# The spatial weight sums of an encoder kernel become a chain of their own, apart from the layer norm

## The chip, the cores and the metric

The kernel runs on one core of one Trainium2 chip. The metric is the device time of one execution in microseconds (us); lower is better. The five engines named in the text are PE (TensorE, the matrix multiply), DVE (VectorE, elementwise work and reductions), ACT (ScalarE, activation functions and copies), POOL (GpSimd, used here almost only to issue transfers) and SP (SyncE, used to issue transfers). Each engine works through its own list of instructions in order: an instruction that waits holds up all that stands behind it on that engine. A transfer (DMA) is issued from the list of an engine and then runs by itself; whoever needs its result waits for its landing.

## The reference: what is computed

A trunk of two residual layers over 512 tokens of 1024 channels. Each layer normalises its input, projects it once, runs three mixers in parallel (a gated linear recurrence, a spatial gating unit, a windowed attention), gates and projects each, and adds the merged result to its input. The change concerns the spatial gating unit alone:

```python
def spatial_gating(u, v, ln_g, ln_b, w_s, b_s):
    vn = layer_norm(v, ln_g, ln_b).reshape(B, L // SG_CHUNK, SG_CHUNK, SG_GROUPS, SG_GW)
    mixed = jnp.einsum('gts,bnsgc->bntgc', w_s, vn) + b_s.T[None, None, :, :, None]
    return u * mixed.reshape(B, L, SG_W)
```

The layer norm has a gain and a bias for each channel, and the mix over positions is linear. So the bias `ln_b` can be taken out of the mix: it contributes, for output position t of group g, `ln_b` times the sum over s of `w_s[g, t, s]`. These sums depend on weights only, not on the input.

## The kernel before, in words

The program is written in Python as one long stream of instructions with tiles taken from pools. A planner then orders the instructions of each engine: it keeps the data dependences, goes by the order of the program as a priority, and may let a later instruction go ahead when an earlier one would still wait by its own estimates. Instructions marked with `pin` keep their order among themselves. The weight loads on SP are pinned.

**The main stream.** PE goes through the weight blocks of a list (`PLAN`). A layer does, in order: the attention's queries (`nat_units(do_q)`, natural layout), its gates and keys, the recurrence's values (`nat_units(do_ia)`), the spatial unit's v (`nat_units(do_vb)`, four token blocks of 24 matmuls, each followed by a GELU of a Square and a Sigmoid on ACT and two operations on DVE, L1041 to L1044), and then for each of four heads h three blocks (query and two forget gates, `main_t`, 24 matmuls each, L520). Each weight block is split into a high part (ACT, L270) and a low part (DVE, L271) before PE may use it.

**Side work.** Between and in the middle of the blocks the program calls `advance(us)`. An advance hands out a credit of `us` to generators. Those in `sides` are served two at a time (`WIDTH = 2`), in turn, until the credit is used up; a generator that yields a number has used that much, and one that yields `None` waits for the next advance. Those in `timed` all run at every advance, ahead of the sides, up to their next `None`; what they use is taken from the same credit. So for a generator in `timed` each `None` is one advance, whatever else goes on. Each of the four token blocks of `do_vb` has two advances (one in its middle, one behind it), and so has each `main_t` block of the heads.

**The attention** is one generator in `sides` (`all_attention`). For each of four query blocks it makes scores on PE (L784 and L785, into the five `ps` slots of PSUM), reads each out with a fused operation on DVE (L786), takes the softmax (ACT L798 and L802, DVE L793 to L809), transposes it on DVE (L816), and sends it through DRAM with two transfers on POOL (L820 and L821). A second generator in `timed` multiplies it with the values eight advances later (L834).

**The layer norm and the weight sums** are one generator before, `ln_v`, which joins `sides` after `do_vb`. Its steps: load the spatial weights into `wsum` (L1054, SP, 256 KB), wait three advances, sum them over s on DVE (L1058), store the 512 sums into a small DRAM tile `sd` (L1060, POOL, 2 KB), load them back spread over all 128 partitions into `wsum` (L1061, POOL, 256 KB), take the mean and variance of v (L1067 and L1068, then the eleven small operations of `rstd`), wait for the next advance, normalise v (L1074), and last add the sums times the bias to the row of output biases `br` (L1079, four operations). `br` is read much later, in `spatial` (L1088). `wsum` holds one of seven slots of the tag `t2` from L1054 to L1079.

Of the kernel before, what the change touches and what calls it, by code (L numbers as in the profile page):

```python
# [18 lines left out]
ALU = mybir.AluOpType  # L19
# [3 lines left out]
P = 128  # L23
# [154 lines left out]
def hybrid_kernel(tc, x, wpk, brow, gainb, pvec, wsp, wsr, trig, amask, imask, out):  # L178
    nc = tc.nc
    from contextlib import ExitStack  # L180

    with ExitStack() as es:
        cp = es.enter_context(tc.tile_pool(name="const", bufs=1))
        wp = es.enter_context(tc.tile_pool(name="wts", bufs=4))
        sb = es.enter_context(tc.tile_pool(name="work", bufs=2))
        pp = es.enter_context(tc.tile_pool(name="psum", bufs=3, space=PSUM))
        dp = es.enter_context(tc.tile_pool(name="spill", bufs=1, space=bass.MemoryType.DRAM))
        build(nc, tc, cp, wp, sb, pp, dp, x, wpk, brow, gainb, pvec, wsp, wsr, trig, amask, imask, out)
# [6 lines left out]
def build(nc, tc, cp, wp, sb, pp, dp, x, wpk, brow, gainb, pvec, wsp, wsr, trig, amask, imask, out):  # L195
    V, S, G, E = nc.vector, nc.scalar, nc.gpsimd, nc.tensor
# [4 lines left out]
    def nm(s):  # L201
        cnt[0] += 1
        return f"{s}_{cnt[0]}"
# [4 lines left out]
    def t2(shape=(P, 512), dt=F32):  # L208
        return sb.tile(list(shape), dt, name=nm("t2"), tag="t2", bufs=N_T2)

    def small(n):
        return sb.tile([P, n], F32, name=nm("sm"), tag="small", bufs=24)
# [4 lines left out]
    def ps_side(shape=(P, 512), dt=F32):  # L217
        return pp.tile(list(shape), dt, name=nm("ps"), tag="ps", bufs=N_PS)
# [56 lines left out]
    def w_next():  # L275
        i = wi[0]
        wi[0] += 1
        w_conv_to(i + 1)
        return his[i], los[i]

    def w_ahead(n, eng=V):
        w_conv_to(wi[0] + n, eng=eng)
        w_load_to(OPERANDS[min(wi[0] + n, len(OPERANDS) - 1)][3])
# [40 lines left out]
    def rstd(ss, n, scale, order=free, small=small):  # L324

        v, y, a = small(n), small(n), small(n)
        order(V.tensor_scalar(v, ss, -0.5 * scale, -0.5 * EPS, ALU.mult, ALU.add))

        magic = float(0x5F3759DF - 0x40400000)
        order(V.tensor_scalar(y.bitcast(I32), v.bitcast(I32), -0.5, magic, ALU.mult, ALU.add))  # L330
        for _ in range(3):
            order(V.tensor_tensor(a, y, y, ALU.mult))
            order(V.tensor_tensor(a, a, v, ALU.mult))
            order(V.scalar_tensor_tensor(y, a, 1.5, y, ALU.add, ALU.mult))
        return y
# [17 lines left out]
    def gate_consts(l, eng):  # L353
        br = cp.tile([P, R_GQ], F32, name=nm("br"), tag="br", bufs=1)
        eng.dma_start(br, brow[l, :R_GQ].partition_broadcast(P))
        ws = cp.tile([P, 4, P], F32, name=nm("ws"), tag="ws", bufs=1)
        eng.dma_start(ws, wsp[l])
        return br, ws
# [118 lines left out]
    def nat_block(units, hth, htl, tb, mid=None, passes=IN_ORDER):  # L477

        po = ps_main()
        nat_part(po, units, hth, htl, tb, passes[:12], True, False)  # L480
        if mid is not None:
            mid()
        nat_part(po, units, hth, htl, tb, passes[12:], False, True)
        return po

    def nat_two(units, hth, htl, tbs, between):

        po = [ps_main() for _ in tbs]
        for n, (i, u) in enumerate(((0, 0), (0, 1), (1, 0), (1, 1), (0, 2), (1, 2), (0, 3), (1, 3))):
            passes = [(2 * u + k, j) for j in range(3) for k in range(2)]  # L490
            nat_part(po[i], units, hth, htl, tbs[i], passes, u == 0, u == 3)
            if n < 7:
                between(n)
        return po
# [32 lines left out]
    timed = []  # L527
# [31 lines left out]
    def advance(us):  # L559
        credit[0] += us  # L560
        waiting = []
        run_timed()
        while sides and credit[0] > 0:
            c = step(waiting)
            if c is None:
                break
            credit[0] -= c
        credit[0] = min(credit[0], 2.0 * us if sides else 0.0)
# [25 lines left out]
    for l in range(L):  # L594
# [4 lines left out]
        lnb = pvc[:, V_LNB + 4 * l : V_LNB + 4 * l + 4]  # L599
# [30 lines left out]
        def nat_units(handler, us, before=None, two=False, passes=IN_ORDER):  # L630
            un = [w_next() for _ in range(4)]
            for tb in range(NT):
                if before is not None:
                    before(tb)
                if two and tb < 2:
                    if tb == 1:
                        pos = nat_two(un, *hN, (0, 1), lambda n: advance(us / 2))
                        for i in range(2):
                            handler(i, pos[i])
                            advance(us / 2)  # L640
                    continue
                po = nat_block(un, *hN, tb, lambda: advance(us), passes if tb == 0 else IN_ORDER)
                if tb == NT - 1:
                    w_ahead(2)
                handler(tb, po)
                advance(us)
# [240 lines left out]
        br, ws = gate_consts(l, nc.sync)  # L887
# [160 lines left out]
                vg.append(m4((P, 2, 512)))  # L1048
            gelu(po, vg[tb // 2][:, tb % 2, :])

        def ln_v():

            wsum = t2((P, 4, P))
            nc.sync.dma_start(wsum, wsr[l])  # L1054
            for _ in range(3):
                yield None
            ss = small(4)
            V.tensor_reduce(ss, wsum, AX, ALU.add)  # L1058
            sd = dp.tile([4, P], F32, name=nm("sd"))
            G.dma_start(sd.rearrange("g t -> t g"), ss)  # L1060
            G.dma_start(wsum.rearrange("p g t -> p (g t)"), sd.rearrange("g t -> (g t)").partition_broadcast(P))  # L1061
            yield 0.5
            mv = small(8)
            mv2 = mv.rearrange("p (n c) -> p n c", c=2)
            for n in range(NT):
                st = small(6)
                V.bn_stats(st, vg[n // 2][:, n % 2, :])  # L1067
                V.bn_aggr(mv2[:, n, :], st)  # L1068
            r = rstd(mv2[:, :, 1], NT, 1.0)
            yield 2.5  # L1070
            yield None
            for n in range(NT):
                v = vg[n // 2][:, n % 2, :]
                V.tensor_scalar(v, v, mv2[:, n, 0:1], r[:, n : n + 1], ALU.subtract, ALU.mult)  # L1074
                yield 0.7

            for g in range(4):
                b = br[:, g * P : (g + 1) * P]
                V.scalar_tensor_tensor(b, wsum[:, g, :], lnb[:, g : g + 1], b, ALU.mult, ALU.add)  # L1079
            yield 0.5  # L1080

        def spatial(g):
            po = ps_side((P, 4, P))
            for n in range(NT):
                E.matmul(po[:, n, :], vg[n // 2][:, n % 2, g * P : (g + 1) * P], ws[:, g, :], start=True, stop=True)  # L1085
            y = t2((P, 4, P))
            bs = br[:, R_BS + g * P : R_BS + (g + 1) * P].unsqueeze(1).broadcast_to((P, 4, P))
            V.scalar_tensor_tensor(y, po, lng[:, g : g + 1], bs, ALU.mult, ALU.add)  # L1088
            u = uz[g // 2][:, g % 2, :]
            V.tensor_tensor(u, u, y.rearrange("p n t -> p (n t)"), ALU.mult)  # L1090
            yield 2.0
# [8 lines left out]

        glas = []
        lnv, spat = ln_v(), [spatial(g) for g in range(4)]
        nat_units(do_vb, 2.6)
        sides.append(lnv)
        for h in range(H):
# [449 lines left out]
```

## Time and profile before

| what | value |
|---|---|
| median of 3 runs | 1073.45 us (1072.95 to 1074.95) |
| the profiled execution's own time | 1074.03 us |
| its span, first to last instruction | 1072.3 us |
| PE busy | 1053.5 us, 98% |
| DVE busy | 819.2 us, 76% |
| ACT busy | 538.1 us, 50% |
| POOL busy | 118.5 us, 11% |
| mean granted TensorE clock | 0.995 |

All times inside the execution are counted from the start of the span. A row of instructions names the line of the kernel, the engine, the operation, and "out<-in" by tile names; `t` stands for a tile of the tag `t2`, `sm` for a small tile, `m` for a large one. In a row of a timeline the brackets at the end tell how long the engine was idle before it and what ended that idle time. In the view of stretches each engine's busy time stands beside the number of its instructions, followed by the clock that TensorE was granted (1.00 is full speed).

### The profile page before, as it was taken

What the parts mean: (1) busy time and instruction counts of PE and PEld (TensorE: products, weight loads), DVE (VectorE), ACT (ScalarE), POOL (GpSimd) and SP (SyncE); (2) the same over time, 40 slices, a digit from 0 to 9 for tenths busy, and PEclk for the clock granted to TensorE, in tenths of its full rate; (3) what the DMA queues carried; (4) which work ended last, traced back from release to release, by engine and by line L of the source; (5) the groups of instructions that cost most, each with busy time, mean ns of one, the idle gap of its engine ahead of it and who ended that gap; (6) DMA issues with size and microseconds to landing.
All of it is one profiled execution on the core that took longest, in us unless ns stands there. A gap on an engine that the chain in (4) does not pass through costs nothing.

```text
span 1072.3 us, 19220 instructions
## 1 busy us (share of the span) xinstructions
PE 1053.5 (98%) x7716; PEld 904.1 (84%) x7716; DVE 819.2 (76%) x1531; ACT 538.1 (50%) x819; POOL 118.5 (11%) x178
## 2 busy tenths in 40 slices
PE   8999989999999999999999999899999999999998
PEld 7888867787899998988878888677778999999886
DVE  6974789968888776578987567897698876775885
ACT  5344757654346543545533367575443464444442
POOL 0230011200001110110012201112000011101000
PEclk9999999999999999999999999899999999999999
DMA  8672446551327866783957424658213378557755
GB/s 311 177 220 95 157 142 231 193 160 60 103 75 159 206 192 162 168 251 112 301 167 231 133 79 157 206 178 260 76 59 120 79 188 219 165 138 193 239 154 141
DMA packets 54281, 178.55 MB, mean 167 GB/s; under 512 B 6320, under 2 KB 10928, under 8 KB 54192
## 3 DMA queue, kind: packets, MB, share of 16 engines
q1 hardware_dynamic: 28944, 100.77, 27.8%
q0 software_dynamic: 23520, 72.37, 26.9%
q10 hardware_dynamic: 1728, 4.20, 1.0%
q8 instruction: 60, 0.98, 0.4%
q14 instruction: 29, 0.24, 0.1%
HBM read 155.28 MB, written 22.02 MB: 165 GB/s over the span
## 4 chain that ended last, share of the span: by engine, by line
PE 79%; issue 12%; DVE 4%; DMA 3%; ACT 1%; POOL 1%; SPq 0%; POOLq 0%; ACTq 0%; DVEq 0%
PE pm L520 37%; PE pm L1189 13%; PE ps L1189 13%; PE pm L473 4%; PE pm L508 2%; DMA wr<-in_wpk 2%; PE ps L834 2%; PE ps L929 1%; DVE wl L271 1%; PE ps L1003 1%; DMA t<-sd 1%; PE ps L1014 1%; PE ps L1085 1%; PE ps L951 1%; PE ps L1018 0%
## 5 line engine op out<-in xcount | busy, mean ns | idle before, releaser
L270 ACT CAST wh<-wr 128x1024 fp32r<-128x1024 f32 x172 | 179.0, 1050 | 194.2 <-PE pm L520 101.5
L271 DVE TENSOR_TENSOR wl<-wr,wh 128x1024 fp32r<-128x1024 f32 x172 | 207.0, 1217 | 66.5 <-issue 23.0
L520 PE MATMUL pm<-hth,wh 128*128 128x512 f32 x448 | 179.1, 400 | 0.0
L520 PE MATMUL pm<-htl,wh 128*128 128x512 f32 x448 | 176.0, 393 | 0.0
L520 PE MATMUL pm<-hth,wl 128*128 128x512 f32 x448 | 174.8, 392 | 0.0
L520 PEld LDWEIGHTS pm<-hth,wl 128*128 128x128 f32 x448 | 84.1, 188 | 17.6
L520 PEld LDWEIGHTS pm<-hth,wh 128*128 128x128 f32 x448 | 84.6, 189 | 16.8 <-ACT m L893 0.2
L520 PEld LDWEIGHTS pm<-htl,wh 128*128 128x128 f32 x448 | 84.5, 189 | 16.1
L520 PE MATMUL pm<-m,wh 128*128 128x512 f32 x256 | 90.8, 393 | 0.0
L473 PE MATMUL pm<-wh,hth 128*128 128x512 f32 x192 | 73.5, 392 | 0.6 <-ACT hth L270 0.5
L473 PE MATMUL pm<-wh,htl 128*128 128x512 f32 x192 | 73.3, 391 | 0.2 <-DVE htl L271 0.2
L473 PE MATMUL pm<-wl,hth 128*128 128x512 f32 x192 | 73.1, 391 | 0.0
L975 DVE TENSOR_TENSOR m<-m,f 128x512 f32<-128x512 f32 x96 | 62.3, 683 | 0.0
L1189 PE MATMUL ps<-hth,wl 128*128 128x256 f32 x192 | 54.5, 284 | 1.5 <-DVE wl L271 1.5
L520 PEld LDWEIGHTS pm<-m,wh 128*128 128x128 f32 x256 | 47.8, 188 | 9.5
L1189 PE MATMUL ps<-hth,wh 128*128 128x256 f32 x192 | 54.6, 284 | 0.0
L1189 PE MATMUL pm<-htl,wh 128*128 128x256 f32 x192 | 54.5, 284 | 0.0
L1189 PE MATMUL pm<-hth,wl 128*128 128x256 f32 x192 | 54.3, 283 | 0.0
L1189 PE MATMUL ps<-htl,wh 128*128 128x256 f32 x192 | 54.3, 283 | 0.0
L1189 PE MATMUL pm<-hth,wh 128*128 128x256 f32 x192 | 54.3, 283 | 0.0
L1189 PE MATMUL pm<-m,wh 128*128 128x256 f32 x288 | 52.8, 284 | 0.5 <-ACT m L1269 0.5
L1189 PE MATMUL ps<-m,wh 128*128 128x256 f32 x288 | 52.6, 283 | 0.0
(268 smaller groups left out, 2461.2 us busy)
## 6 DMA issues: line engine op xcount, KB each, us to landing
wr<-in_wpk SPq DMA_DIRECT2D x172, 512.0 KB, 4.5
hold<-in_wpk POOLq DMA_DIRECT2D x40, 512.0 KB, 7.0
pd<-m POOLq DMA_DIRECT2D x20, 512.0 KB, 4.4
m<-pd POOLq DMA_DIRECT2D x20, 512.0 KB, 5.0
wr<-in_wpk POOLq DMA_DIRECT2D x16, 512.0 KB, 7.2
m<-in_x SPq DMA_DIRECT2D x8, 512.0 KB, 6.4
m<-xd POOLq DMA_DIRECT2D x16, 256.0 KB, 6.8
m<-in_wpk POOLq DMA_DIRECT2D x8, 512.0 KB, 7.2
```

Of the source, the lines that this page charges most:

```text
L270: order(S.copy(hi_dst, src))
L271: order(eng.tensor_tensor(lo_dst, src, hi_dst.bitcast(F32), ALU.subtract))
L473: E.matmul(po, a, b[:, o : o + 512], start=first and n == 0, stop=last and n == len(passes) - 1)
L508: E.matmul(po[:, k, :], a, b[:, o : o + 256], start=n == 0, stop=n == 23)
L520: E.matmul(po, s, m, start=n == 0, stop=n == 3 * nk - 1)
L834: E.matmul(po[64 * g : 64 * g + 64], vC[:, k0 + kb, 64 * g : 64 * g + 64], pt[:, :, 128 * g : 128 * g + 128], start=kb == 0, stop=kb == le ...
L929: E.matmul(cb[p0 : p0 + 32, slot, j // 4, :], kk(32 * j), qq(32 * j), start=True, stop=True, tile_position=(0, p0),)
L951: E.matmul(dg[p0 : p0 + 32, j // 4, f0 : f0 + 32], kx[:, 32 * j : 32 * j + 32] if m == 16 else k_op(32 * j, m), q_op(32 * jq, m), start=Tr ...
L975: V.tensor_tensor(v, v, custom(ff, of, ([sd, 2], [2, ng], [0, m])), ALU.mult)
L1003: E.matmul(st[:, c, :], kts[d][:, c, :], v_of(c + d), start=True, stop=True)
L1014: E.matmul(po[:, t, :], pm[:, t, :], v_of(t), start=True, stop=False)
L1189: E.matmul(banks[g][:, r, :], a, b, start=not onto and (r, kt, n) == (0, 0, 0), stop=kt == 3 and n == 2, skip_group_check=onto is not None ...
```

## The change

`ln_v` is cut in two. The weight sums become a generator of their own, `output_bias`, and it joins `timed` before `do_vb` instead of `sides` after it. At its first advance (in the middle of the first token block of v) it loads the weights; at its fourth it sums them and stores the sums; at its eighth it issues the load that spreads them; at its sixteenth it adds them to the bias row. `ln_v` keeps the layer norm, joins `sides` where it did, and now begins with the statistics at its first turn, where it had three `None` before. No instruction is added or dropped.

```diff
-        def ln_v():
+        def output_bias():
 
             wsum = t2((P, 4, P))
             nc.sync.dma_start(wsum, wsr[l])
+            yield 0.0
             for _ in range(3):
                 yield None
             ss = small(4)
             V.tensor_reduce(ss, wsum, AX, ALU.add)
             sd = dp.tile([4, P], F32, name=nm("sd"))
             G.dma_start(sd.rearrange("g t -> t g"), ss)
+            yield 0.3
+            for _ in range(4):
+                yield None
             G.dma_start(wsum.rearrange("p g t -> p (g t)"), sd.rearrange("g t -> (g t)").partition_broadcast(P))
+            for _ in range(8):
+                yield None
+            for g in range(4):
+                b = br[:, g * P : (g + 1) * P]
+                V.scalar_tensor_tensor(b, wsum[:, g, :], lnb[:, g : g + 1], b, ALU.mult, ALU.add)
             yield 0.5
+
+        def ln_v():
             mv = small(8)
             mv2 = mv.rearrange("p (n c) -> p n c", c=2)
             for n in range(NT):
...
                 V.tensor_scalar(v, v, mv2[:, n, 0:1], r[:, n : n + 1], ALU.subtract, ALU.mult)
                 yield 0.7
 
-            for g in range(4):
-                b = br[:, g * P : (g + 1) * P]
-                V.scalar_tensor_tensor(b, wsum[:, g, :], lnb[:, g : g + 1], b, ALU.mult, ALU.add)
-            yield 0.5
-
...
         lnv, spat = ln_v(), [spatial(g) for g in range(4)]
+        timed.append(output_bias())
         nat_units(do_vb, 2.6)
         sides.append(lnv)
```

## The prediction

> **What bounds the kernel now.** I read the page first: what is busy, and what the chain that ended last is made of.
>
> ```profile
> span 1072.3 us, 19220 instructions
> PE 1053.5 (98%) x7716; PEld 904.1 (84%) x7716; DVE 819.2 (76%) x1531; ACT 538.1 (50%) x819; POOL 118.5 (11%) x178
> PE 79%; issue 12%; DVE 4%; DMA 3%; ACT 1%; POOL 1%; SPq 0%; POOLq 0%; ACTq 0%; DVEq 0%
> ```
>
> PE bounds it, so a change pays only where PE idles or is slowed: 18.8 us of idle in all, 1072.3 less 1053.5. The chain holds 3% of DMA. Followed in order of time through the first layer, it crosses the weight sums:
>
> ```profile
> 134.73 0.75 POOL sd L1060
> 135.48 8.20 issue
> ...
> 143.70 4.88 DMA t<-sd
> ...
> 148.60 0.35 DVE br L1079
> ...
> 150.61 0.44 PE ps L784
> ```
>
> The sums are stored at 134.73, lie in flight for 8.2 us, are spread by a second transfer of 4.88 us, and DVE starts its bias operations only then. Behind them PE resumes. The table of waits says who stood still, in layer 0 (128 to 171 us) and layer 1 (656 to 700):
>
> ```profile
> DVE br L1079 <- DMA t<-sd: 5.0, 1, 5.0
> PE ps L784 <- DVE sm L786: 4.0, 1, 4.0
> ...
> DVE br L1079 <- DMA t<-sd: 5.0, 1, 5.0
> PE ps L784 <- DVE sm L786: 4.7, 1, 4.7
> ```
>
> DVE waits 5.0 us for the transfer. Queued behind L1079 stand the read-outs of the attention's scores, L786; without them no `ps` slot comes free, so PE stops at its next score matmul, L784, and with it the in-order stream of L520. The stretches around the stop show that it costs more than its length:
>
> ```profile
> 146.40:150.60 4.20, 0.17 (x1) 0.00 (x0) 2.00 (x12) 1.85 (x2) 0.22 (x1) 1.00 0.91 301
> 150.60:157.60 7.00, 6.99 (x28) 4.52 (x29) 7.00 (x27) 0.00 (x0) 1.90 (x4) 0.76 0.80 238
> 157.60:165.00 7.40, 7.40 (x34) 6.10 (x33) 7.30 (x17) 6.42 (x19) 0.71 (x1) 1.00 0.87 288
> ...
> 674.20:679.10 4.90, 0.20 (x1) 0.00 (x0) 1.98 (x12) 2.50 (x4) 0.66 (x2) 0.78 0.73 268
> 679.10:686.00 6.90, 6.87 (x25) 4.31 (x26) 6.90 (x27) 0.00 (x0) 2.27 (x4) 0.66 0.80 233
> ```
>
> The columns: length, then PE, weight load, DVE, ACT and POOL busy, granted clock, DMA share, GB/s. After each stop PE is busy but at a clock of 0.76 or 0.66 for some 7 us.
>
> **The change part by part.** *The stop.* In layer 0: 4.2 less 0.17 is 4.03 us idle, and 7.00 x (1 - 0.76) = 1.68 us of lost clock. In layer 1: 4.9 - 0.2 = 4.7, and 6.9 x (1 - 0.66) = 2.35. Together 4.03 + 1.68 + 4.7 + 2.35 = 12.8 us. This is what the change can take away here. [...]
>
> *Where the chain goes.* The ends of v's token blocks are seen in ACT's first read of each, that of the second head's query in L1108:
>
> ```profile
> 104.43 0.58 ACT L1041 ACTIVATE m<-pm 128x512 f32<-128x512 f32 x1
> 110.25 0.58 ACT L1041 ACTIVATE m<-pm 128x512 f32<-128x512 f32 x1
> 114.44 0.60 ACT L1041 ACTIVATE m<-pm 128x512 f32<-128x512 f32 x1 [0.17 <-PE pm L473]
> 122.78 0.60 ACT L1041 ACTIVATE m<-pm 128x512 f32<-128x512 f32 x1 [0.51 <-PE pm L473]
> ...
> 146.38 0.59 ACT L1108 COPY t<-pm 128x512 f32<-128x512 f32 x1 [2.47 <-PE pm L520]
> ```
>
> Two advances to a block: the fourth lies at or before 110.25, the eighth at 122.8, the sixteenth at about 146.4 (six for head 0's three blocks, two for head 1's query). What the chain's parts take:
>
> ```profile
> L1054 SPq DMA_DIRECT2D t<-in_wsr x2: 425/425/425, 77.4 to 604.3; - x2
> L1058 DVE TENSOR_REDUCE sm<-t x2: 634/634/635, 133.8 to 662.3; 128x4 f32<-128x512 f32 x2
> ...
> L1067 DVE BATCH_NORM_STATS2 sm<-m x8: 649/662/674, 137.6 to 671.5; 128x6 f32<-128x512 f32 x8
> ...
> L1079 DVE SCALAR_TENSOR_TENSOR br<-t,pvc,br x8: 321/348/352, 148.6 to 678.1; 128x128 f32<-128x128 f32 x8
> t<-sd POOLq DMA_DIRECT2D x2, 256.0 KB, 4.8
> sd<-sm POOLq DMA_DIRECT2D x2, 2.0 KB, 8.7
> ```
>
> The reduction moves from 133.8 to about 111. Its store then lands near 111 + 1 + 8.7 = 121, and the load, issued at about 122.8, near 127.6. The bias operations' turn comes at 146.4: about 19 us to spare, where the old order was 5.0 short. Even if the planner pulls them ahead by 15 us nothing waits. I take the whole stop as gone. [...]
>
> *The cost in the new place.* Same instructions, so DVE's 0.63 + 4 x 0.35 = 2.0 us a layer only move; SP's 0.425 us was already issued at 77.4, 45 us ahead of its place in the program, between weight loads, and stays so. For POOL the neighbours are:
>
> ```profile
> 82.25 1.26 POOL L697 DMA_DIRECT2D t<-xd x2 [1.97 <-DMA xd<-t]
> 115.05 0.57 POOL L820 DMA_DIRECT2D pd<-m  x1 [31.55 <-DVE m L816]
> 116.18 0.56 POOL L820 DMA_DIRECT2D pd<-m  x1 [0.56 <-DVE m L816]
> ...
> 119.63 0.77 POOL L821 DMA_DIRECT2D m<-pd  x1 [0.60 <-DMA pd<-m]
> ...
> 154.07 2.22 PE L834 MATMUL ps<-m,t 128*64 128x512 f32 x8
> ```
>
> The store finds POOL free (31 us idle). If the planner puts the spreading load directly behind it, POOL waits until 121 and holds up these transfers of the attention (two L820, two L821) by at most 6 us; their reader, L834, runs on PE at 154. Cost nothing; without that cover it would be 6 us. In return the pair for the second query block no longer stands behind L1061.
>
> *The layer norm starts three advances earlier*, at 125 instead of 134, beside the attention. DVE has room there:
>
> ```profile
> 122.50:134.00 11.50, 11.50 (x53) 9.57 (x52) 6.09 (x12) 10.86 (x24) 0.00 (x0) 1.00 0.63 212
> 134.00:158.00 24.00, 19.97 (x87) 15.08 (x87) 19.00 (x58) 11.64 (x15) 4.91 (x8) 0.93 0.44 128
> 158.00:170.00 12.00, 12.00 (x55) 9.96 (x54) 11.90 (x23) 10.27 (x23) 0.87 (x2) 1.00 0.60 206
> ```
>
> It works 6.09 of 11.5 us, while the stretch behind is full but for the 5.0 us wait. The attention cedes the credit of about two advances (2.5 + 4 x 0.7 = 5.3 us) and gets it back by the time at which the old layer norm would have ended. Bounds for a layer: the reduction and the four statistics (0.63 + 4 x 0.66 = 3.3 us) leave the full stretch, so at best 3.3 us; at worst the attention's 5.3 us of delay reach PE. I take nothing, being nearest to the row of 6.09 in 11.5. The `t2` slot is held from 77.4 or later to 147, where it was held to 150: nothing.
>
> Sum: 12.8 us less. The profiled time 1074.03 becomes 1061.2; the median stands 0.58 lower, so 1060.7 for the median. The edges: idle alone (8.7) leaves 1064.7; half of the 3.3 us in each layer on top (16.1) makes 1057.
>
> **The rivals.** *DVE sets the pace instead.* In 134 to 158 DVE has 19.0 us of work in 24, PE at full clock 24 - 4.03 - 1.68 = 18.3. If none of that DVE work leaves the stretch, only 5.0 us a layer come back: 10.0, so 1063.4; with a short wait left at the scores, up to 1069. For it: 11.9 of 12 us busy behind. Against: the reduction and four statistics do leave it. [...]
>
> *The gain is given back, or the planner keeps the old place.* The chain waits for weight loads later on:
>
> ```profile
> 351.83 7.15 DMA wr<-in_wpk
> ...
> 879.65 6.73 DMA wr<-in_wpk
> ```
>
> If these came at their old times, the gain would drown there: about 1073. Against it: behind the stop PE is busy throughout (7.40 of 7.40 us, 12.00 of 12.00), and these loads wait for buffers that its own progress frees. Against the second half: the load L1054, issued 45 us ahead of its place, shows that the planner moves such steps forward, not back.
>
> *Slower: L1079 is pulled close behind its transfers.* The planner orders DVE by its own idea of how long a transfer takes. In the old order:
>
> ```profile
> 133.80 0.63 DVE L1058 TENSOR_REDUCE sm<-t 128x4 f32<-128x512 f32 x1
> ...
> 148.60 0.35 DVE L1079 SCALAR_TENSOR_TENSOR br<-t,pvc,br 128x128 f32<-128x128 f32 x1 [5.00 <-DMA t<-sd]
> ```
>
> From the reduction's end (134.4) to DVE's arrival at L1079 (148.6 - 5.0 = 143.6) lay 9.2 us of DVE work; the transfers need 14.2. If the planner, finding L1079 ready by its reckoning, sets it about 5 us behind the reduction in v's blocks, DVE stops for 9 us there, PE by the present ratio (5.7 to 7.1 us for 5.0) for about 10 to 12. That is 20 to 24 for both layers in place of 12.8: 1081 to 1085. It decides from 9.2 us of distance downwards. For it: L1079 already stands ahead of the last L1068 and of all L1074, which the program has before it. Against: it moved by one advance or so, not by eight.
>
> **How the numbers follow.** The forecast 0.62, DVE's pace or another partial gain 0.17, given back or unmoved 0.10, slower 0.11. The likeliest gives 1060.7, its own range 1057 to 1065. To leave out 2 in 10 the range takes in the partial gains and most of the unmoved case: 1056.5 to 1072.5. 0.2% is about 2.1 us, about what a measurement can tell from no change. Faster by more: 0.62 + 0.17 = 0.79; within: 0.10; slower: 0.11.
>
> **What would show it.** The reduction near 111 us, its store on POOL in the idle time before 115; no wait of L1079 for the spreading load; no PE idle of 4 us at 146 and 674; a clock of 1.00 throughout 150 to 158; then everything behind about 6 us earlier in layer 0 and 13 in layer 1. It is wrong if DVE waits at L1079 in another place, if PE waits for L786 as long as before with DVE full, or if the starts near 300 us have not shifted.

## The result and the profile after

The changed kernel takes 1063.29 us (1062.48 to 1065.04, 4 runs) beside 1073.38 us (1072.95 to 1074.95, 4 runs) of the kernel before: a ratio of 0.9906, 95% interval 0.9888 to 0.9923. It is faster by 10.1 us; 12.8 were forecast. A repeat on another chip gave 0.9918 (0.9899 to 0.9937). The profiled run took 1063.95 us.

The page of the changed kernel (span, busy time and share of each engine, shares of the chain that ended last):

```profile
span 1062.2 us, 19231 instructions
PE 1049.1 (99%) x7716; PEld 902.1 (85%) x7716; DVE 819.8 (77%) x1531; ACT 537.4 (51%) x819; POOL 118.6 (11%) x178
PE 89%; DVE 5%; ACT 2%; DMA 2%; issue 1%; SPq 0%; DVEq 0%; ACTq 0%
```

The page alone splits the gain. PE's idle time was 1072.3 - 1053.5 = 18.8 us and is 1062.2 - 1049.1 = 13.1 us: 5.7 us less. PE's busy time fell from 1053.5 to 1049.1 us for the same 7716 matmuls: 4.4 us, read here as lost clock that came back. Together 10.1 us. Profiled runs of experiments 8 and 9 at a clock of 1.00 have PE busy for 1050.5 and 1049.2 us, so this split holds to about 1 us.

In the table of waits no wait of DVE for the spreading load (`t<-sd`) is left. PE's waits for the score read-outs went from 8.8 us (4.0 and 4.7) to 2.7 us. The row of the changed kernel gives the total, the number of waits and the longest:

```profile
PE ps L784 <- DVE sm L786: 2.7, 2, 1.4
```

The stretches of the changed kernel (length, then PE, weight load, DVE, ACT and POOL busy, granted clock, DMA share, GB/s); the first and the last hold the places of the old stops:

```profile
134.00:158.00 24.00, 24.00 (x109) 18.81 (x108) 23.96 (x64) 15.06 (x21) 3.94 (x6) 1.00 0.57 195
158.00:170.00 12.00, 12.00 (x59) 9.97 (x57) 9.47 (x18) 11.97 (x27) 0.56 (x1) 1.00 0.39 156
170.00:190.00 20.00, 17.74 (x258) 12.04 (x256) 18.14 (x52) 14.15 (x30) 3.39 (x5) 1.00 0.67 223
...
656.00:686.00 30.00, 29.96 (x136) 23.49 (x136) 28.36 (x73) 23.03 (x42) 3.93 (x6) 1.00 0.60 204
```

Where PE worked 19.97 of 24 us at a clock of 0.93, it now works 24.00 of 24 at 1.00. The first stop is gone whole, and its clock with it. But from 170 to 190 us PE now idles 2.26 us, and 1.39 of them are a **second stop**, smaller and some 25 us later (the other 0.87 us stand ahead of L929, with no cause that the profile shows). The kernel before had no idle time there:

```profile
170.00:190.00 20.00, 20.00 (x240) 14.13 (x238) 17.00 (x45) 14.64 (x33) 3.39 (x5) 1.00 0.73 245
```

What the chain does in its new place, from the timelines of POOL and DVE in the changed kernel (start, length, instruction; in brackets the idle time before it and what ended it):

```profile
111.60 0.80 POOL L1062 DMA_DIRECT2D sd<-sm  x1 [27.89 <-DVE sm L1060]
120.86 0.56 POOL L1066 DMA_DIRECT2D t<-sd  x1 [8.47 <-DMA sd<-sm]
121.42 1.08 POOL L820 DMA_DIRECT2D pd<-m  x2
```

```profile
127.82 1.13 DVE L1071 SCALAR_TENSOR_TENSOR br<-t,pvc,br 128x128 f32<-128x128 f32 x4
...
134.30 0.64 DVE L1079 BATCH_NORM_STATS2 sm<-m 128x6 f32<-128x512 f32 x1
```

```profile
t<-sd POOLq DMA_DIRECT2D x2, 256.0 KB, 4.6
```

The store goes out at 111.60. POOL waits for it 8.47 us, and the spreading load is issued at 120.86. By the row of its transfers (size, median us to landing) it takes 4.6 us, so it lands at about 125.5. The bias operations run at 127.82: no wait, but only 2.3 us to spare. The statistics of the layer norm begin at 134.30 in layer 0, where they began at 137.6.

The second stop, in both layers, as the timeline of PE shows it in the changed kernel:

```profile
171.62 0.35 PE L784 MATMUL ps<-m,m 128*128 128x256 f32 x1 [1.39 <-DVE sm L786]
693.96 0.36 PE L784 MATMUL ps<-m,m 128*128 128x256 f32 x1 [1.33 <-DVE sm L786]
```

Here the score matmuls of the fourth query block wait for their first read-out. On DVE that read-out stands behind the softmax of the third block. In layer 0 the chain to it goes through ACT; the timelines of before, then of after:

```profile
158.79 0.62 ACT L798 ACTIVATE scores<-scores,sm 128x384 f32<-128x384 f32 x1 [0.20 <-DVE sm L795]
```

```profile
154.75 1.06 ACT L270 CAST wh<-wr 128x1024 fp32r<-128x1024 f32 x1 [5.56 <-PE pm L520]
...
157.12 0.62 ACT L798 ACTIVATE scores<-scores,sm 128x384 f32<-128x384 f32 x1
```

```profile
153.39 0.17 DVE L795 TENSOR_SCALAR sm<-sm 128x8 f32<-128x8 f32 x1
...
160.47 1.23 DVE L271 TENSOR_TENSOR wl<-wr,wh 128x1024 fp32r<-128x1024 f32 x1 [1.98 <-issue]
162.17 0.17 DVE L803 TENSOR_TENSOR sm<-sm,sm 128x8 f32<-128x8 f32 x1 [0.47 <-ACT sm L802]
...
162.62 3.19 DVE L809 TENSOR_SCALAR scores<-scores,sm 128x384 f32<-128x384 f32 x8
...
170.98 0.48 DVE L786 CUSTOM_DVE_ANT_0 scores<-ps,am,rows 128x256 f32<-128x256 f32 x1
```

In layer 0 of the changed kernel DVE has the third block's scores ready for the exponentials at 153.56 (L795), but in ACT's list a weight cast (L270) stands ahead of them, and it waits 5.56 us for PE to free its buffer. The exponentials start at 157.12, only 1.67 us earlier than before (158.79), while PE has gained some 5.4 us by then (24.00 us of full clock from 134 to 158, against 19.97 x 0.93). Division, transposes and read-out follow in a row up to 170.98. PE, freed from its first stop, has caught up with this chain.

Layer 1 is another case. There ACT is ready first, and DVE releases the exponentials:

```profile
679.22 0.62 ACT L798 ACTIVATE scores<-scores,sm 128x384 f32<-128x384 f32 x1 [0.47 <-DVE sm L795]
```

DVE works 28.36 of 30 us from 656 to 686 (above), and up to the read-outs at 693.32 it waits for ACT only 0.68 us. So the second stop of layer 1 is set mostly by DVE's own work.

### The profile page after: what moved, and what is told of

Its sections match the earlier page's. It is cut to its first block, busy times and chain, and to the rows that moved or that the text cites. A ratio compares the mean times of both kernels' runs of the same rounds, so it can differ in the third digit from the quotient of the medians.

```text
span 1062.2 us, 19231 instructions
## 1 busy us (share of the span) xinstructions
PE 1049.1 (99%) x7716; PEld 902.1 (85%) x7716; DVE 819.8 (77%) x1531; ACT 537.4 (51%) x819; POOL 118.6 (11%) x178
## 4 chain that ended last, share of the span: by engine, by line
PE 89%; DVE 5%; ACT 2%; DMA 2%; issue 1%; SPq 0%; DVEq 0%; ACTq 0%
PE pm L520 40%; PE ps L1197 13%; PE pm L1197 13%; PE pm L473 11%; PE pm L508 2%; PE ps L834 2%; PE ps L929 1%; DMA wr<-in_wpk 1%; DVE wl L271 1%; PE ps L1003 1%; PE ps L784 1%; PE ps L785 1%; PE ps L1014 1%; PE ps L1092 1%; DMA m<-in_x 1%
## 5 line engine op out<-in xcount | busy, mean ns | idle before, releaser
L270 ACT CAST wh<-wr 128x1024 fp32r<-128x1024 f32 x172 | 179.5, 1052 | 210.0 <-PE pm L520 131.5
L271 DVE TENSOR_TENSOR wl<-wr,wh 128x1024 fp32r<-128x1024 f32 x172 | 207.6, 1219 | 70.3 <-issue 31.1
```

Of the source, the lines that this page charges most:

```text
L270: order(S.copy(hi_dst, src))
L271: order(eng.tensor_tensor(lo_dst, src, hi_dst.bitcast(F32), ALU.subtract))
```

## The experiments

**1. The bias operations later, everything else as before.** The kernel before, with eight advances of waiting ahead of L1079.

```diff
+            for _ in range(8):
+                yield None
             for g in range(4):
                 b = br[:, g * P : (g + 1) * P]
```

> The kernel before with eight more waits of one advance ahead of its bias operations (L1081 here), all else as before. In the planned order of DVE the first of the four then stands only some six small operations further back, the other three about forty rows further, behind the scores' read-outs. Theory A (what counts is whether DVE, in the planner's order, reaches the first bias operation before the spreading load has landed; the number of advances in the program counts only through that): DVE still stops there, for about 4.5 us instead of 5.0, and the time stays near the one before, 1070 to 1073 us. Theory B (the waits that the program makes between transfer and use bring the gain): the stop goes and the time falls to about 1063.

Measured: 1069.67 us (1068.64 to 1071.02, 10 runs), ratio 0.9978 (0.9968 to 0.9987), profiled span 1068.2 us. The waits of this kernel:

```profile
DVE br L1081 <- DMA t<-sd: 4.2, 2, 2.4
PE pm L520 <- ACT m L893: 3.3, 1, 3.3
...
PE ps L784 <- DVE sm L333: 2.2, 2, 1.3
PE ps L784 <- DVE sm L786: 1.6, 1, 1.6
```

Eight advances in the program moved the first of the four operations by only some 3 us in DVE's list (the wait falls from 10.0 to 4.2 us over both layers). The first stop shrinks from 8.8 to 2.2 us, and new stops of 3.3 and 1.6 us return most of it. The time is just below the first forecast and far above the second: a later reader alone is worth about a fifth of the change.

**2. The load twice: the wait made longer.** The kernel before with its spreading load issued a second time.

```diff
             G.dma_start(wsum.rearrange("p g t -> p (g t)"), sd.rearrange("g t -> (g t)").partition_broadcast(P))
+            G.dma_start(wsum.rearrange("p g t -> p (g t)"), sd.rearrange("g t -> (g t)").partition_broadcast(P))
```

> The kernel before with the spreading load issued twice into the same tile, the second behind the first. Theory A: the data are there 4.8 to 5.3 us later, DVE waits about 9.5 us in each layer, PE's stop grows by as much, and the time rises by 10 to 13 us to 1083 to 1086. Rival (the stop of PE has another cause, such as POOL's attention transfers behind the spreading load or the five score slots, and DVE's wait only lies beside it): the time moves by less than 3 us.

Measured: 1086.52 us (1085.29 to 1087.2, 4 runs), ratio 1.0129 (1.0112 to 1.0146).

```profile
DVE br L1080 <- DMA t<-sd: 17.8, 2, 9.1
PE ps L784 <- DVE sm L333: 15.9, 2, 8.2
PE pm L520 <- ACT m L893: 3.3, 1, 3.3
```

7.8 us more of waiting on DVE (17.8 against 10.0) give 7.1 us more at PE's first stop (15.9 against 8.8) and a new stop of 3.3. In all PE idles 11.9 us more (30.7 against 18.8) and is busy for 1.2 us longer; the median rises by 14.5 us, a little over the forecast. The wait of the bias operations does set PE's stop, nearly one for one.

**3. The same chain, begun behind v.** The changed kernel, with the chain joined to `timed` after the blocks of v.

```diff
-        timed.append(output_bias())
         nat_units(do_vb, 2.6)
+        timed.append(output_bias())
```

> The changed kernel with its chain of the sums joined to the timed generators behind v's blocks instead of ahead of them: a chain of its own, but started where the old one was. In DVE's planned order the bias operations stand behind the second block's score read-outs and the normalisation, which the changed kernel reaches at about 153 us, when a load issued near 144 has landed. Theory A: no wait at the bias operations, 1061 to 1065 us like the changed kernel. Rival (the early start in v's blocks is what brings the gain): DVE still stops some us near 144 and the time stays above 1068.

Measured: 1076.95 us (1072.99 to 1079.56, 10 runs; the profiled one is the fastest), ratio 1.0041 (1.0027 to 1.0055): slower than the kernel before, though the first stop is gone here too (24.00 of 24 us at 1.00 from 134 to 158). Against the first forecast the bias operations wait again in layer 0:

```profile
161.08 0.61 DVE L1071 SCALAR_TENSOR_TENSOR br<-t,pvc,br 128x128 f32<-128x128 f32 x2 [2.84 <-DMA t<-sd]
```

In layer 1 they do not wait, but PE stops for longer. From its chain and its timelines of ACT and PE there:

```profile
670.54 12.09 DMA wr<-in_wpk
```

```profile
679.18 1.05 ACT L270 CAST wh<-wr 128x1024 fp32r<-128x1024 f32 x1 [8.39 <-DMA wr<-in_wpk]
682.72 1.05 ACT L270 CAST wh<-wr 128x1024 fp32r<-128x1024 f32 x1 [2.49 <-PE pm L520]
```

```profile
695.16 0.80 PE L520 MATMUL pm<-hth,wh 128*128 128x512 f32 x1 [5.59 <-ACT m L893]
700.09 0.55 PE L784 MATMUL ps<-m,m 128*128 128x256 f32 x1 [2.43 <-DVE sm L786]
```

In one cast ACT waits 8.39 us for its weights. The load for the next cast crosses the chain's store and load, is in flight for 12.09 us and lands at 682.63, just ahead of that cast. Softmax and gates queue behind. So the long waits alone do not make the gain: the place does. Whether the chain's transfers made these weight loads slow was asked in experiment 7.

**4. The chain apart, but without long waits.** The changed kernel without the four and the eight advances.

```diff
             G.dma_start(sd.rearrange("g t -> t g"), ss)
             yield 0.3
-            for _ in range(4):
-                yield None
             G.dma_start(wsum.rearrange("p g t -> p (g t)"), sd.rearrange("g t -> (g t)").partition_broadcast(P))
-            for _ in range(8):
-                yield None
```

> The changed kernel without its last two groups of waits: the spreading load is issued right behind the store, and the bias operations stand right behind the load (the four and the eight waits are left out). The planner then sets the bias operations ahead of the third GELU and all read-outs of the second block's scores, which DVE reaches at about 117 us, some 8 us before the load can have landed (125.5). Theory A: DVE waits about 8 us in each layer, PE stops for about as long and runs slow afterwards, the time rises by 14 to 20 us over the changed kernel, to 1077 to 1083. Theory that only the separation from the layer norm matters: as the changed kernel, 1061 to 1065.

Measured: 1081.91 us (1081.17 to 1084.6, 4 runs), ratio 1.0095 (1.0077 to 1.0112). Its waits, and the first bias operations on its DVE:

```profile
DVE br L1067 <- DMA t<-sd: 15.9, 2, 8.2
PE ps L784 <- DVE sm L786: 16.9, 4, 7.4
```

```profile
124.65 1.14 DVE L1067 SCALAR_TENSOR_TENSOR br<-t,pvc,br 128x128 f32<-128x128 f32 x4 [7.73 <-DMA t<-sd]
```

DVE arrives at 124.65 - 7.73 = 116.9, ahead even of the store's landing in the changed kernel (120.86), and waits 7.73 us. This is the prediction's slower rival, at its price. In this place the twelve `None` are what buys the gain.

**5. The distance measured.** The changed kernel with its spreading load issued three times over.

```diff
             G.dma_start(wsum.rearrange("p g t -> p (g t)"), sd.rearrange("g t -> (g t)").partition_broadcast(P))
+            G.dma_start(wsum.rearrange("p g t -> p (g t)"), sd.rearrange("g t -> (g t)").partition_broadcast(P))
+            G.dma_start(wsum.rearrange("p g t -> p (g t)"), sd.rearrange("g t -> (g t)").partition_broadcast(P))
```

> The changed kernel with the spreading load issued three times over in place of once, into the same tile from the same store. Each further load is issued when the one before it has landed, so that the sums are there about 9.4 us later (4.6 us of transfer for each, and GpSimd's start). Theory A (the trace of the changed kernel: the bias operations start at 127.82, 2.3 us after the landing at 125.5): they wait for the load, 6 to 7.5 us in each layer. VectorE stands idle for 1.20 and 3.14 us behind them in the changed kernel, which covers 4.3 us; 2 to 3 us are left and come out in the stops at the score read-outs of the fourth block, and the attention's first transfers, which stand behind the loads in GpSimd's queue, go 8 us later: 1065 to 1072 us. Rival, the prediction's distance of 19 us between the load's landing and the operations: no wait of the bias operations for the load at all, and a time within 1.5 us of the changed kernel's 1063 us.

Measured: 1077.35 us (1076.61 to 1079.58, 4 runs), ratio 1.0053 (1.0034 to 1.0071). The third load's issue on POOL, the bias operations on DVE, and PE's waits:

```profile
131.89 0.55 POOL L1068 DMA_DIRECT2D t<-sd  x1 [2.85 <-DMA t<-sd]
```

```profile
137.15 1.14 DVE L1073 SCALAR_TENSOR_TENSOR br<-t,pvc,br 128x128 f32<-128x128 f32 x4 [9.23 <-DMA t<-sd]
```

```profile
PE pm L520 <- DVE m L1044: 8.8, 2, 4.4
```

DVE arrives at 137.15 - 9.23 = 127.92, as in the changed kernel, and waits 9.2 us in each layer. With 19 us to spare it would not have waited at all; the distance of 2.3 us is confirmed. The wait is longer than the 6 to 7.5 us expected, because the second load, issued at 125.19 beside two transfers of the attention, took 6.2 us to land, where 4.6 were reckoned, and POOL issued the third only then, at 131.89. The time missed the expected 1065 to 1072 with it.

**6. The layer norm held back.** The changed kernel with the old three advances ahead of the statistics.

```diff
         def ln_v():
+            for _ in range(3):
+                yield None
             mv = small(8)
```

> The changed kernel with the three waits of one advance put back ahead of the layer norm's statistics, so that only the chain of the sums has moved. Theory A (the sums and their transfers are the whole effect): within 2 us of the changed kernel. Rival (the layer norm's earlier start carries a part, by filling DVE's free time ahead of the tight stretch): slower than the changed kernel by 3 us or more.

Measured: 1068.26 us (1066.16 to 1070.39, 7 runs), ratio 0.9967 (0.9953 to 0.9981); the repeat of the changed kernel on the same chip took 1063.18 (1062.12 to 1064.96). Of that repeat was expected:

> The changed kernel once more, beside the others of this call: 0.989 to 0.992 of the kernel before.

The first stop stays gone, but 5.1 us go of the 8.4 by which that repeat lies below the kernel before (1071.62 us beside them), as the rival had it. With the layer norm held back, the moved chain brings only 3.4 us. The timeline of PE, and two of the stretches; the profiled run took 1070.32 us and is one of the slower of the seven:

```profile
171.83 0.36 PE L784 MATMUL ps<-m,m 128*128 128x256 f32 x1 [1.89 <-DVE sm L786]
...
694.33 0.50 PE L520 MATMUL pm<-hth,wh 128*128 128x512 f32 x1 [3.31 <-ACT m L893]
696.49 0.55 PE L784 MATMUL ps<-m,m 128*128 128x256 f32 x1 [0.73 <-DVE sm L786]
```

```profile
170.00:190.00 20.00, 18.17 (x252) 11.79 (x253) 17.64 (x52) 11.91 (x27) 3.38 (x5) 0.91 0.65 227
...
686.00:710.00 24.00, 19.96 (x226) 12.55 (x225) 19.78 (x48) 17.20 (x39) 3.93 (x6) 0.86 0.57 197
```

The layer norm's normalisation comes later (in layer 1 at 678.16, in the changed kernel at 670.79). In layer 0 the second stop grows to 1.89 us. In layer 1 PE stops for 3.31 us, until ACT's gates (L893) come, and for 0.73 us at the scores. In these stretches the clock falls to 0.91 and 0.86, where the changed kernel keeps 1.00, and there most of the time goes: in all PE idles only 0.8 us more than in the changed kernel (13.9 against 13.1), but it is busy for 5.5 us longer with the same matmuls (1054.6 against 1049.1). In layer 1, ACT also waited for weights ahead of the exponentials:

```profile
679.46 1.05 ACT L270 CAST wh<-wr 128x1024 fp32r<-128x1024 f32 x1 [4.58 <-DMA wr<-in_wpk]
```

So how much of the 5.1 us is DVE's later work, and how much this load, stays open.

**7. Are the chain's transfers harmful in a late place?** The changed kernel with a second store and spreading load behind the statistics, which nothing reads.

```diff
+            sd2 = dp.tile([4, P], F32, name=nm("sd2"))
+            G.dma_start(sd2.rearrange("g t -> t g"), mv[:, 0:4])
+            dum = t2((P, 4, P))
+            G.dma_start(dum.rearrange("p g t -> p (g t)"), sd2.rearrange("g t -> (g t)").partition_broadcast(P))
```

> The changed kernel with two transfers added in each layer that nobody reads, of the same kind and near the place of the old ones: four columns of the statistics stored as 512 single numbers, and that spread over 128 partitions into a tile of its own. POOL's list is held up behind them as it was before; DVE waits for neither. Theory A (only DVE's wait cost time): within 2 us of the changed kernel. Theory F (the transfers themselves harm in that place, by holding up POOL's attention transfers and slowing the weight loads there, as the chain started behind v's blocks did in layer 1, where a weight load took 12.09 us): slower than the changed kernel by 4 to 12 us, with new stops of PE near 170 and 690 us.

Measured: 1066.12 us (1063.99 to 1068.24, 4 runs), ratio 0.9946 (0.9925 to 0.9966), 2.9 us over the changed kernel measured beside it (1063.18); between the two forecasts. On ACT a cast now waits for its weights where it waited 0.22 us before:

```profile
152.32 1.06 ACT L270 CAST wh<-wr 128x1024 fp32r<-128x1024 f32 x1 [4.49 <-DMA wr<-in_wpk]
```

The weight loads issued from 140 to 160 us took 7.4 us (median) where the changed kernel's took 4.5; but without the chain (experiment 9) they took 6.1, so the slower loads are not shown to be the transfers' doing. The price is in any case far below the some 14 us by which experiment 3 lies over the changed kernel. How much of those is due to the transfers, and how much to the order that the planner chose there, stays open.

**8. The second stop taken away.** The changed kernel without the division of the third query block's scores (L809), so that this block's weights are not normalised.

```diff
-                V.tensor_scalar_mul(p, p, rc[:, h : h + 1])
+                if qb != 2:
+                    V.tensor_scalar_mul(p, p, rc[:, h : h + 1])
```

> The changed kernel without the division of the third query block's softmax weights by their sums (eight operations of DVE, 3.2 us in each layer), which stand right ahead of the small stops of PE that are left (1.39 us near 171, 1.33 near 693). Theory D (DVE's pace sets these stops): both vanish, 2.5 to 3 us faster than the changed kernel. Theory E (ACT's list sets them: exponentials, casts, table loads and gates in one row): the one of layer 1 stays, where DVE waited 0.7 us for ACT's gates just before; at most 1.5 us faster.

Measured: 1060.23 us (1059.86 to 1060.81, 4 runs), ratio 0.9891 (0.9877 to 0.9906), 2.95 us under the changed kernel measured beside it, and no run of the one reaches into the range of the other. No wait at L784 is left, in layer 1 as in layer 0, and layer 1's stretch is full:

```profile
686.00:710.00 24.00, 24.00 (x316) 17.23 (x315) 19.98 (x55) 18.16 (x37) 3.10 (x5) 1.00 0.60 199
```

This is the forecast of the theory that DVE's pace sets both stops; the theory of ACT's list had the one of layer 1 stay. The third block's softmax on DVE carries the second stop: without its 3.19 us of division a layer, the 2.7 us come back.

**9. What the chain still costs.** The changed kernel with no chain at all; the bias rows lack the layer norm's term.

```diff
-        timed.append(output_bias())
```

> The changed kernel without the chain of the sums: no load of the weights for it, no reduction, no store, no spreading load, and no bias operations, so that the bias rows lack the layer norm's term. It gives what the chain still costs in its new place. It issues in each layer one reduction (0.63 us of VectorE), four bias operations (1.39 us together), and three transfers (the last two took 9.0 and 4.6 us). Theory A: in its new place the chain costs nearly nothing beside VectorE's 2.0 us per layer, which lie ahead of the stop at the score read-outs of the fourth block; without them this stop shrinks by up to 1.4 us per layer: 1060 to 1063.5 us, that is 0 to 3 us below the changed kernel. Rival: the transfers and the operations of the chain still hold the layer up in a way that no wait of the bias operations shows (the list, the queues): 1058 us or less.

Measured: 1062.26 us (1061.75 to 1062.92, 4 runs), ratio 0.9909 (0.9893 to 0.9924). By the ratios (0.9906 and 0.9918 with the chain) nothing can be told: in its new place the chain costs about nothing. The profiled run has one second stop in place of two. In layer 0, where it has none, ACT's exponentials were not held back:

```profile
153.21 0.62 ACT L798 ACTIVATE scores<-scores,sm 128x384 f32<-128x384 f32 x1 [0.21 <-DVE sm L795]
```

They start as soon as L795 releases them, 3.9 us ahead of the changed kernel's 157.12. In layer 1 DVE releases them too, as in the changed kernel, and the stop of 1.33 us stays.

**10 and 11. DVE relieved of the normalisation.** In one kernel GpSimd does the four normalising operations of a layer, in the other ScalarE.

```diff
-                V.tensor_scalar(v, v, mv2[:, n, 0:1], r[:, n : n + 1], ALU.subtract, ALU.mult)
+                G.tensor_scalar(v, v, mv2[:, n, 0:1], r[:, n : n + 1], ALU.subtract, ALU.mult)
```

> The changed kernel with the four normalising operations of each layer (128x512 numbers each) on GpSimd in place of VectorE. Theory D (behind the change VectorE sets the pace at the fourth block's score read-outs, 1.4 us per layer): VectorE has about 2 us less to do ahead of that place, the second stop goes as it did without the third block's division: 1060 to 1062 us. Rival: GpSimd, which issues the attention's transfers in the same stretch, is held up by these operations, the transfers come later, and the time is 1064 us or more.

```diff
+            nb = small(4)
+            V.scalar_tensor_tensor(nb, mv2[:, :, 0], -1.0, r, ALU.mult, ALU.mult)
...
-                V.tensor_scalar(v, v, mv2[:, n, 0:1], r[:, n : n + 1], ALU.subtract, ALU.mult)
+                S.activation(v, v, AF.Identity, bias=nb[:, n : n + 1], scale=r[:, n : n + 1])
```

> The changed kernel with the four normalising operations of each layer on ScalarE (an identity with scale and bias, and one small operation more on VectorE that makes the bias). Theory D: VectorE has some 2 us less ahead of the fourth block's read-outs, the second stop goes: 1060 to 1062 us. Rival: ScalarE is itself nearly full in this stretch (23.96 of 24 us PE, with ScalarE's own exponentials and casts behind the layer norm); the exponentials come later by the added operations, about 3 us per layer, and the read-outs with them: 1064 us or more.

Measured: on GpSimd 1061.26 us (1060.82 to 1062.01, 4 runs), ratio 0.9900 (0.9884 to 0.9915); on ScalarE 1068.62 us (1066.69 to 1071.13, 10 runs), ratio 0.9972 (0.9961 to 0.9982). GpSimd's is in the range of the first theory, but its interval overlaps that of the changed kernel, so it is not shown to be faster. The waits at L784 fell only from 2.7 to 2.0 us for 2 us less of DVE work in each layer. ScalarE's is slower, as its rival had it (the 23.96 of 24 us in that forecast is DVE's row of 134 to 158; ACT works 15.06 us there, and 11.97 of 12 only from 158 to 170); first ACT, then PE of that kernel:

```profile
154.60 2.93 ACT L1088 ACTIVATE m<-m,sm,sm 128x512 f32<-128x512 f32 x4
...
159.13 0.62 ACT L798 ACTIVATE scores<-scores,sm 128x384 f32<-128x384 f32 x1
```

```profile
170.64 0.50 PE L520 MATMUL pm<-hth,wh 128*128 128x512 f32 x1 [3.31 <-ACT m L893]
```

The exponentials start 2 us later than in the changed kernel (159.13 against 157.12), the gates behind them (L893) come too late, and PE stops for 3.31 us. Side by side, the start of the third block's exponentials in layer 0 and PE's idle time there: without the chain 153.21 and none at L784; changed 157.12 and 1.39 us; layer norm held back 157.92 and 1.89; on ScalarE 159.13 and 3.31, with the gates then ending it. In these four the second stop of layer 0 goes with ACT's place for the exponentials, but two others show that this is not all of it: on GpSimd they start at 154.32, on DVE's release, and 0.87 us are left; in experiment 3 they start at 152.54 and 1.42 us are left, and there DVE had waited 2.84 us for the spreading load. What all have in common is DVE's chain of softmax and transposes ahead of the read-outs. That ACT's list holds it up in layer 0 is read from the trace, not shown by a run of its own. Setting the exponentials ahead of the cast L270 in ACT's list by hand was not tried, and why the planner puts the cast first in some lists and not in others stays open.

## Why the prediction was right or wrong

**The time: 2.6 us too low.** 1063.29 lies inside the likeliest case's own range, 1057 to 1065. The direction and the mechanism, the stop of PE behind L1079, held (experiments 2 and 4).

**The stop, 12.8 us: right.** Its place is full at a clock of 1.00 in both layers. The clock's share was put at 1.68 + 2.35 = 4.03 us; PE's busy time fell by 4.4. That moving the chain is enough to bring all of this back did not hold, as the next paragraph says.

**The step that failed: "I take nothing" for what the earlier stretch does to DVE and ACT.** The sum has no term for a second stop, and the changed kernel has one of 1.39 + 1.33 = 2.72 us, which is the shortfall: idle of 8.73 us removed, 2.72 of it returned, leaves 6.0, and 5.7 were measured. In layer 0 the prediction did not follow ACT's list, where the third block's exponentials stand behind a cast that waits for PE. In layer 1 DVE is nearly full (28.36 of 30 us from 656 to 686) and releases them itself. The same "nothing" was wrong for the layer norm: its three advances are worth 5.1 us (experiment 6), though its statistics begin only 3.3 us earlier in layer 0 (134.30, not the 125 of the prediction); in layer 1 the normalisation moved from 684.49 to 670.79. The bounds given there, 3.3 us of gain to 5.3 of loss in a layer, held it; the value taken from them did not. So that the sum came within 2.6 us is in part luck: with the layer norm held back, the same chain in the same place brought 3.4 us, not 12.8: PE still lost idle time and clock behind other stops.

**"About 19 us to spare": wrong, without harm.** The store's issue (111.60 against "near 111" and its 1 us), its landing (by 120.86 against 121) and the load's (125.5 against 127.6) came about as worked out. The bias operations did not wait for their advance at 146.4: the planner set them at 127.82, 18.6 us ahead. "Even if the planner pulls them ahead by 15 us nothing waits" fell short by those few us; the distance is 2.3 us, and experiment 5 shows what lies behind it.

**The cost in the new place, nothing: right.** POOL did wait for the store (8.47 us), and the attention's pair went out at 121.42 instead of 115.05, the 6 us of the prediction. No wait of PE answers to it, and without the chain the time is the same within the measurement (experiment 9).

**The rivals.** *DVE sets the pace instead* had the size almost exactly (10.0 us, 1063.4) and much of the mechanism: a short wait at the scores remains (1.39 and 1.33 us, with the clock at 1.00 in both stretches), and in layer 1 it is DVE's own work that PE catches up with. In layer 0 DVE is not full: it works 9.47 of 12 us from 158 to 170 and stands idle for 1.98 us ahead of L271, and by the rows ACT's list comes in. Not every stretch with a short wait kept its clock: the one with a wait of 1.89 us had 0.91 (experiment 6). *The gain given back later* fell. *Slower* fell for this kernel, and is real: without the long waits the kernel takes some 19 us more than the changed one (experiment 4).

## What to carry to other kernels

A planner that goes by its own estimate of a transfer's time may set its reader close behind it, wherever the program has it; waits in the program move the reader only in part (eight advances gave 3 us in one place, and sixteen left 2.3 us to spare in the other), so the distance is read from the trace and not from the program. When a stop is removed, follow every engine's list up to the next place where PE depends on it: an engine that waits in the wrong order (here ACT, whose exponentials came 1.67 us earlier where PE had gained some 5.4), or has no time to spare (here DVE, busy for 28.36 of 30 us), does not keep up, and there the next stop lay. Work that starts earlier in a full stretch is not free to ignore: here three advances of a small layer norm carried over half the gain (5.1 of 8.4 us).

## What was not expected of the hardware

**VectorE's divisions took longer beside GpSimd's work.** With the normalisation on GpSimd (its four operations from 154.35 for 10.13 us), the eight divisions of the same stretch took longer. From 150 to 170 us, first the changed kernel, then this one (total and mean ns):

```profile
L809 DVE TENSOR_SCALAR scores<-scores,sm 128x384 f32<-128x384 f32 x8 | 3.2, 472 | 0.0
```

```profile
L809 DVE TENSOR_SCALAR scores<-scores,sm 128x384 f32<-128x384 f32 x8 | 4.4, 622 | 0.0
```

In layer 0, 1.2 us of the 2 us taken from DVE went back that way. In layer 1, where GpSimd had finished before the divisions began (its last operation started at 676.1 and its longest took 3.6 us, the divisions start at 681.51), they took 472 ns as ever. Why they took longer in layer 0 no run here shows.

**The clock beside short stops of PE.** In the changed kernel the stretches with stops of 1.39 and 1.33 us had a clock of 1.00 (170 to 190 and 686 to 710 us). In experiment 6 the stretch with stops of 3.31 and 0.73 us had 0.86 (686 to 710 us), and the stretch with one of only 1.89 us had 0.91 (170 to 190 us). Why the clock fell beside so short a stop stays open.
